# A decoder trunk with product-key experts on one core: stores of what ScalarE has written, issued by ScalarE instead of SyncE

## The chip, the cores and the metric

The kernel runs on one core of one Trainium2 chip. The metric is the time of one execution on the device in microseconds (us); less is better. PE is the matmul engine TensorE, DVE is VectorE, ACT is ScalarE, POOL is GpSimd and SP is SyncE, which has no arithmetic and here issues transfers only. Each of these engines works through a list of instructions of its own in the written order, and an instruction that waits holds everything behind it on that engine, the issue of transfers included.

## The reference

One layer of a decoder on 1024 tokens of width 1024, in float32. Two token mixers run beside each other (differential attention, and attention over 256 positions that an indexer selects), their outputs are gated and projected, an attention over 256 memory tokens is added, and then comes the channel mixer, in which most of the time goes:

```python
q = (hf @ w_q).reshape(n, PEER_HEADS, 2, PEER_HALF)              # 8 heads
sc = jnp.einsum('nhcd,hckd->nhck', q, sub_keys)                  # 2 x 128 keys a head
s_top, i_top = lax.top_k(sc, PEER_TOPK)                          # 16 + 16
...                                                              # best 16 of their sums
idx = best_i.reshape(n, PEER_HEADS * PEER_TOPK)                  # 128 of 16384 experts a token
g = jax.nn.softmax(best_s, axis=-1)
...
a = jnp.einsum('cd,ced->ce', hc, u[ic])
a = jax.nn.gelu(a, approximate=False) * gc
return jnp.einsum('ce,ced->cd', a, v[ic])
```

A residual sum and an rms norm end it.

## The kernel before

The tokens lie in eight blocks of 128, in two groups of four. Each group goes through the same phases: P (projections, from which some results are spilled to HBM), T (both attentions; a side lane "fill" computes the gates and, in the first group, the keys and values of the memory), G and O (gating and output product), M (memory attention) and R (the experts' scores, stored to HBM as pq). After phase R of the first group its blocks 0 to 3 are served by gathers: POOL fetches 128 rows of u and 128 rows of v per block by index, 512 each in all, and DVE multiplies them (L1031, L1050). These gathers are spread over the rest of the program as a lane of their own.

The blocks of the second group, 4 to 7, are not gathered. `dense` runs all 128 tiles of 128 experts over them. It has two stages.

The early stage makes the first 48 U products. For each, SP loads a tile uraw (512 KB, three buffers), ACT and DVE split it into a high and a low part uT (L106, L107, two buffers), PE does 24 matmuls into one accumulator (L129 to L131), ACT applies the gelu (two buffers) and the result is stored to ga (256 KB, L1219). Beside it runs the lane "weights", which finds for each of the four blocks the chosen experts ("route"), transposes them (L1124, L1125), makes bit codes of them (L1144, L1145) and then, four tokens at a time in 32 iterations a block, the table of all experts' weights: a product dot, oh by ACT (L1161), ah by DVE (L1163), a product out, and a copy by ACT into wbuf (L1169). A wbuf holds half a block (64 tokens), and there are two. Each half is stored to Wd by eight stores of 512 KB (L1177), put into a list when the half is done and taken from it one by one in the steps that follow, or all at once where the next half of a block needs it.

The main stage then goes through all 128 expert tiles in groups of four. `group` loads the weights wl from Wd (L1237), and c from ga (L1241) or makes it by a U product, and multiplies the two; `second` loads V (vraw, L1256), splits it and makes the second product (L129 to L131 again, into kept and out).

A scheduler sets the order of the instructions on each engine from the order of the code, the lanes' times and its own costs, and lays down which buffers wait for what. Before the change every transfer of `dense` and nearly all others are issued by SP. A Wd store is put behind the last u load that was issued when it was recorded (`issue_after`). Eight semaphores mark the end of transfers; SP's and ACT's transfers take them in turn, and an issue also waits for the transfer that had the same semaphore before.

Of the kernel before, what the change touches and what calls it, by code (L numbers as in the profile page):

```python
# [78 lines left out]
class K:  # L79
# [245 lines left out]
    def phase_P(self, g, st, hp, hT):  # L325
        nc, a = self.nc, self.a
        blks = self.blks
        w_in = a["w_in"][0]
        with ExitStack() as ctx:
# [5 lines left out]
            for i, b in enumerate(blks):  # L335
                x = pp.tile([P, D], F32, name="x", bufs=X_BUFS[g])
                nc.sync.dma_start(x, a["x"][0, b * P:(b + 1) * P])
                h = pp.tile([P, D], F32, name="h", bufs=X_BUFS[g])
# [121 lines left out]

            def use_dav(i, b, o):
                t = copy(o, 512)
                nc.sync.dma_start(self.dav[b], t)

            self.daq = self.scratch([4, 2, 2, 64, self.GT], f"daq{g}")
            self.dsq = self.scratch([self.GB, 64, 2, 2, 512], f"dsq{g}")
# [38 lines left out]
    def gates(self, g, hT):  # L505

        nc = self.nc
        for c in range(0, 16, 2):
            yield from self.fill(self.a["w_in"][0], KD, C_GATE + c * P, 256, 2, self.by_col(hT), self.GT, len(hT) == 1)
            for j in range(2):  # L510
                t = self.fp.tile([P, 512], F32, name="fout", bufs=2)[:, :self.GT]
                nc.scalar.activation(t, self.filled[j][:, :self.GT], AF.Tanh, bias=self.gb[:, c + j:c + j + 1], scale=0.5)
                self.gate[g, c + j] = self.scratch([P, self.GT], f"G{g}_{c + j}")
                nc.sync.dma_start(self.gate[g, c + j], t)

    def rope_view(self, d, s, b, groups):
        nc = self.nc
# [273 lines left out]
    def memory_kv(self):  # L791
        nc, w = self.nc, self.a["w_mem_kv"][0]
        self.mkd = self.scratch([P, 4, 256], "mkd")
        self.mvd = [self.scratch([P, 512], f"mvd{i}") for i in range(2)]
        for c in range(0, 4, 2):
            yield from self.fill(w, KD, c * P, 256, 2, self.by_col(self.memT), 256)
            for j in range(2):
                t = self.fp.tile([P, 512], F32, name="fout", bufs=2)
                nc.scalar.activation(t[:, :256], self.filled[j][:, :256], AF.Copy)
                nc.sync.dma_start(self.mkd[:, c + j], t[:, :256])  # L800
        yield from self.fill(w, KD, 512, 512, 2, lambda k, x, j: ([t[:, k, j * P:(j + 1) * P] for t in self.memT], x), 512)
        for i in range(2):
            t = self.fp.tile([P, 512], F32, name="fout", bufs=2)
            nc.scalar.activation(t, self.filled[i], AF.Copy)
            nc.sync.dma_start(self.mvd[i], t)

    def queries_M(self, g, x1, q, hp):
        nc, a = self.nc, self.a
# [54 lines left out]
    def phase_R(self, g, x1, rh, fp):  # L863
        nc, a = self.nc, self.a
        with ExitStack() as ctx:
# [17 lines left out]
            for half in range(2):  # L883
                po = self.product([(a["peer_w_q"][0], half * 512, 512)], KD, 512, self.by_column(T), self.GT, 4)
                for j in range(0, 4, 2):
# [6 lines left out]
                    for i in range(self.GB):  # L892
                        o = self.acc()
                        for hh in range(2):
                            nc.tensor.matmul(o[:, hh * 256:(hh + 1) * 256], qs[hh][:, i * P:(i + 1) * P],
                                             keysT[:, h + hh], start=True, stop=True)
                        so = rp.tile([P, 512], F32, name="so", bufs=3)
                        nc.scalar.activation(so, o, AF.Copy)
                        nc.sync.dma_start(self.pq[self.blks[i]][h // 2], so)
                    self.pace.tick(4 * 0.9)  # L900


# [206 lines left out]
    def weights(self, blks):  # L1109

        nc = self.nc
# [5 lines left out]
        for j, b in enumerate(blks):  # L1117
# [30 lines left out]
            for n0 in range(0, P, 4):  # L1148
# [24 lines left out]
                if m + 4 == H:  # L1173
                    for e0 in range(0, P, 16):
                        def store(e0=e0, at=2 * j + n0 // H, wbuf=wbuf):
                            with self.tc.issue_after(self.last_load):
                                nc.sync.dma_start(self.Wd[at, :, e0:e0 + 16], wbuf[:, e0:e0 + 16])  # L1177
                        stores.append(store)
        while stores:
            stores.pop(0)()  # L1180
# [2 lines left out]
    def dense(self, psum, early):  # L1183
# [5 lines left out]
        with ExitStack() as ctx:  # L1189
# [20 lines left out]
            with ExitStack() as c2:  # L1210
# [3 lines left out]
                for e in range(early):  # L1214
# [1 line left out]
                    t = self.wb.tile([P, 512], F32, name="gelu", bufs=2)  # L1216
                    nc.scalar.activation(t, o, AF.Gelu)
                    ga[e] = self.scratch([P, 512], f"ga{e}")
                    nc.sync.dma_start(ga[e], t)  # L1219
                self.pace.drain("weights")  # L1220
            self.route_ctx.close()
            psum = self.psum_phase(psum, "ps3", A_BUFS)
# [199 lines left out]
```

## Time and profile before

| | |
|---|---|
| Time, median of three runs | 3506.32 us (3500.16, 3506.32, 3507.83) |
| The profiled execution | 3504.34 us |
| Its span (first to last instruction) | 3502.6 us |
| Mean granted clock of PE | 0.932 of full speed |
| PE busy | 3011.4 us, 86% of the span |
| DVE busy | 2853.1 us, 81% |
| ACT busy | 1398.2 us, 40% |
| POOL busy | 1389.4 us, 40% |
| Transfers issued by SP (the hardware queue) | 401.94 MB, 33.7% of the span of the 16 transfer engines |
| Gathers by POOL | 560.01 MB, 45.3% |

The first 640 us are the first group, 640 to about 1640 us the second, 1640 to 2241 us the early stage of `dense`, and the rest is its main stage. The issuing of transfers does not count as an engine's busy time. Where a row tells of a wait, the time in brackets is the engine's idle time just before the instruction, and behind the arrow stands what ended it.

### The profile page before, as it was taken

How to read it: one execution, taken by the hardware profiler on the slowest of the kernel's cores; microseconds unless marked ns; L12 is line 12 of the kernel's file. 1: busy time of each engine (PE TensorE's matmuls, PEld its weight loads, DVE VectorE, ACT ScalarE, POOL GpSimd, SP SyncE). 2: the span in 40 equal slices, each digit the busy share in tenths (PEclk: the TensorE clock that was granted, in tenths of full speed). 3: DMA queues.
4: the chain of work that ended last, by engine and by line, in shares of the span. 5: the costliest groups of instructions: out<-in, count | busy, mean ns of one | idle time of the engine just before them, and what ended most of it. 6: DMA issues, size and time to landing. Idle time of an engine off the chain costs nothing. (4 is left out here: it accounts for less than half of the span.)

```text
span 3502.6 us, 42276 instructions
## 1 busy us (share of the span) xinstructions
PE 3011.4 (86%) x13234; PEld 2283.0 (65%) x13234; DVE 2853.1 (81%) x6623; ACT 1398.2 (40%) x2537; POOL 1389.4 (40%) x1122
## 2 busy tenths in 40 slices
PE   8999888798687698676899895588899999999997
PEld 7777766553355575455677674466677888787886
DVE  6656554598878979888999888677789999899998
ACT  5756344245666441322546465222222222222222
POOL 0010000011245246653122665424457665777665
PEclk9999989899899799788999998799999999999999
DMA  4575544335799579897486999999999999999997
GB/s 138 163 186 133 169 138 142 124 121 192 210 296 297 143 262 362 296 327 277 149 296 219 364 377 346 369 302 319 307 340 368 380 381 367 364 364 387 376 381 285
DMA packets 394210, 964.64 MB, mean 275 GB/s; under 512 B 36713, under 2 KB 146049, under 8 KB 392577
## 3 DMA queue, kind: packets, MB, share of 16 engines
q0 software_dynamic: 155264, 560.01, 45.3%
q1 hardware_dynamic: 238720, 401.94, 33.7%
q8 instruction: 104, 1.70, 0.2%
q14 instruction: 122, 0.99, 0.1%
HBM read 871.64 MB, written 90.18 MB: 275 GB/s over the span
## 5 line engine op out<-in xcount | busy, mean ns | idle before, releaser
L1028 POOL DMA_INDIRECT rows<-in_peer_u_dram,ii x512 | 673.8, 1316 | 920.8 <-DVE rows L1031 377.0
L1044 POOL DMA_INDIRECT rows<-in_peer_v_dram,ii x512 | 651.0, 1272 | 438.9 <-DVE h3s L1050 286.2
L1050 DVE SCALAR_TENSOR_TENSOR h3s<-rows,wexp,h3s 128x1024 f32<-128x1024 f32 x508 | 651.1, 1282 | 38.9 <-DMA rows<-in_peer_v_dram,ii 29.4
L1031 DVE SCALAR_TENSOR_TENSOR rows<-rows,h3s 128x1024 f32<-128x1024 f32 x512 | 611.9, 1220 | 81.5 <-DMA rows<-in_peer_u_dram,ii 80.0
L129 PE MATMUL acc<-fT,uT 128*128 128x512 f32 x1024 | 415.7, 406 | 46.3 <-ACT uT L106 26.0
L131 PE MATMUL acc<-fT,uT 128*128 128x512 f32 x1024 | 413.5, 404 | 11.8 <-DVE uT L107 11.5
L130 PE MATMUL acc<-fT,uT 128*128 128x512 f32 x1024 | 410.2, 401 | 0.0
L106 ACT ACTIVATE c<-wl 128x512 fp32r<-128x512 f32 x128 | 80.2, 631 | 817.1 <-PE out L130 407.8
L143 POOL TENSOR_TENSOR rstd<-msq,mhalf 128x1 f32<-128x1 f32 (+1 forms) x42 | 35.6, 847 | 597.4 <-DVE msq L141 578.6
L129 PEld LDWEIGHTS acc<-fT,uT 128*128 128x128 f32 x1024 | 197.0, 192 | 92.2 <-ACT uT L106 26.8
L131 PEld LDWEIGHTS acc<-fT,uT 128*128 128x128 f32 x1024 | 197.0, 192 | 66.7 <-DVE uT L107 21.0
L130 PE MATMUL kept<-v,c 128*128 128x512 f32 x512 | 206.2, 405 | 38.8 <-DVE v L107 38.8
L129 PE MATMUL kept<-v,c 128*128 128x512 f32 x512 | 202.6, 402 | 37.6 <-ACT v L106 36.2
L106 ACT ACTIVATE uT<-uraw 128x1024 fp32r<-128x1024 f32 x128 | 135.5, 1059 | 245.4 <-PE acc L130 135.0
L130 PEld LDWEIGHTS acc<-fT,uT 128*128 128x128 f32 x1024 | 197.2, 193 | 39.2
L107 DVE TENSOR_TENSOR w<-wraw,w 128x512 fp32r<-128x512 f32 (+1 forms) x176 | 116.7, 680 | 117.9 <-ACT w L106 111.2
L129 PE MATMUL out<-v,c 128*128 128x512 f32 x512 | 203.9, 398 | 9.7 <-DVE accu L1274 9.7
L131 PE MATMUL kept<-v,c 128*128 128x512 f32 x512 | 203.4, 397 | 0.0
L130 PE MATMUL out<-v,c 128*128 128x512 f32 x512 | 203.0, 396 | 0.0
L131 PE MATMUL out<-v,c 128*128 128x512 f32 x512 | 202.8, 396 | 0.0
L562 ACT ACTIVATE junk<-W,xb 128x384 bf16<-128x384 f32 (+5 forms) x186 | 163.8, 881 | 77.3 <-DVE xb L560 67.8
L127 PE MATMUL acc<-wraw,hT 128*128 128x512 f32 (+1 forms) x384 | 168.4, 592 | 14.1 <-ACT tok L349 10.9
(361 smaller groups left out, 6691.5 us busy)
## 6 DMA issues: line engine op xcount, KB each, us to landing
uraw<-in_peer_ut_dram SPq DMA_DIRECT2D x128, 512.0 KB
vraw<-in_peer_v_dram SPq DMA_DIRECT2D x128, 512.0 KB
Wd<-wbuf SPq DMA_DIRECT2D x64, 512.0 KB
wl<-Wd SPq DMA_DIRECT2D x64, 512.0 KB
wraw<-in_w_in_dram SPq DMA_DIRECT2D x40, 512.0 KB
fraw<-in_w_in_dram SPq DMA_DIRECT2D x32, 512.0 KB
wraw<-in_w_out_dram SPq DMA_DIRECT2D x24, 512.0 KB
ga<-gelu SPq DMA_DIRECT2D x48, 256.0 KB
```

The lines of the kernel that those rows point to most:

```text
L106: self.nc.scalar.activation(hi, src, AF.Copy)
L107: self.last_dve = self.nc.vector.tensor_tensor(lo, src, hi.bitcast(F32), op=OP.subtract).ins
L127: self.last_pe = nc.tensor.matmul(out, l[0], r[0], start=start, stop=stop).ins
L129: nc.tensor.matmul(out, l[0], r[0], start=start, stop=False)
L130: nc.tensor.matmul(out, l[0], r[1], start=False, stop=False)
L131: self.last_pe = nc.tensor.matmul(out, l[1], r[0], start=False, stop=stop).ins
L143: nc.gpsimd.tensor_tensor(r, v, self.mhalf[:, :n], op=OP.pow)
L562: nc.scalar.activation(junk[:, :(b + 1) * P], self.W[b], AF.Sign, bias=xb[:, j:j + 1].bitcast(F32), accum_out=s[:, j:j + 1])
L1028: nc.gpsimd.indirect_dma_start(out=u, out_offset=None, in_=a["peer_u"][0], in_offset=bass.IndirectOffsetOnAxis(ap=ii[:, j:j + 1], axis=0))
L1031: nc.vector.scalar_tensor_tensor(u, u, 1.0, h3, op0=OP.mult, op1=OP.mult, accum_out=aa[:, j:j + 1])
L1044: nc.gpsimd.indirect_dma_start(out=v, out_offset=None, in_=a["peer_v"][0], in_offset=bass.IndirectOffsetOnAxis(ap=r["ii"][:, j:j + 1], axi ...
L1050: nc.vector.scalar_tensor_tensor(o, v, w[:, j:j + 1], o, op0=OP.mult, op1=OP.add)
```

## The change

190 stores whose data ACT has written are issued by ACT (`nc.scalar`) instead of SP (`nc.sync`): 8 of dav, 32 of the gates, 4 and 2 of the memory's keys and values, 32 of pq, 64 of Wd and 48 of ga. The Wd stores lose their place behind the last u load. The spilled queries and keys, x2, h3 and the output stay with SP, and so do all loads. Nothing that is computed changes.

```diff
             def use_dav(i, b, o):
                 t = copy(o, 512)
-                nc.sync.dma_start(self.dav[b], t)
+                nc.scalar.dma_start(self.dav[b], t)
...
                 self.gate[g, c + j] = self.scratch([P, self.GT], f"G{g}_{c + j}")
-                nc.sync.dma_start(self.gate[g, c + j], t)
+                nc.scalar.dma_start(self.gate[g, c + j], t)
...
                 nc.scalar.activation(t[:, :256], self.filled[j][:, :256], AF.Copy)
-                nc.sync.dma_start(self.mkd[:, c + j], t[:, :256])
+                nc.scalar.dma_start(self.mkd[:, c + j], t[:, :256])
...
             nc.scalar.activation(t, self.filled[i], AF.Copy)
-            nc.sync.dma_start(self.mvd[i], t)
+            nc.scalar.dma_start(self.mvd[i], t)
...
                         nc.scalar.activation(so, o, AF.Copy)
-                        nc.sync.dma_start(self.pq[self.blks[i]][h // 2], so)
+                        nc.scalar.dma_start(self.pq[self.blks[i]][h // 2], so)
...
                         def store(e0=e0, at=2 * j + n0 // H, wbuf=wbuf):
-                            with self.tc.issue_after(self.last_load):
-                                nc.sync.dma_start(self.Wd[at, :, e0:e0 + 16], wbuf[:, e0:e0 + 16])
+                            nc.scalar.dma_start(self.Wd[at, :, e0:e0 + 16], wbuf[:, e0:e0 + 16])
                         stores.append(store)
...
                     ga[e] = self.scratch([P, 512], f"ga{e}")
-                    nc.sync.dma_start(ga[e], t)
+                    nc.scalar.dma_start(ga[e], t)
```

The scheduler writes the order anew, so the change shows in three places of the early stage. In the listings a number behind a name tells apart the tiles of one name, x2 or x8 stands for so many rows alike, and after the change the lines from L1177 on have numbers one lower.

First listing, before: SP's queue at the second half of the third block (wbuf_17520), up to the last of five u loads.

```order
L1196 DMA uraw_18246<-in_peer_ut_dram 128x1024
L1177 DMA Wd_13635<-wbuf_17520 128x1024 x2
L1219 DMA ga43_17980<-gelu_17978 128x512
L1177 DMA Wd_13635<-wbuf_17520 128x1024 x3
L1219 DMA ga44_18068<-gelu_18066 128x512
L1177 DMA Wd_13635<-wbuf_17520 128x1024 x3
L1219 DMA ga45_18143<-gelu_18141 128x512
L1196 DMA uraw_21052<-in_peer_ut_dram 128x1024
L1196 DMA uraw_21098<-in_peer_ut_dram 128x1024
L1196 DMA uraw_21146<-in_peer_ut_dram 128x1024
```

The same place of SP's queue after the change, and on to the first loads of the main stage.

```order
L1195 DMA uraw_18246<-in_peer_ut_dram 128x1024
L1195 DMA uraw_21052<-in_peer_ut_dram 128x1024
L1195 DMA uraw_21098<-in_peer_ut_dram 128x1024
L1195 DMA uraw_21146<-in_peer_ut_dram 128x1024
L1195 DMA uraw_21189<-in_peer_ut_dram 128x1024
L1195 DMA uraw_21395<-in_peer_ut_dram 128x1024
L1236 DMA wl_18902<-Wd_13635 128x8x128
L1240 DMA c_18904<-ga0_13695 128x512
```

The stores have left the queue: the u loads follow each other, and the two u loads of the main stage that stood between the last Wd stores and wl before (uraw_21441, uraw_21486) now come behind the first loads of V.

Second listing, before: ACT in the last block, where its first half (wbuf_18422) is done and the second (wbuf_18655) begins.

```order
L1169 ACTIVATE wbuf_18422<-out_18641 128x4x128
L1161 ACTIVATE oh_18674<-dot_18670,m6_13636 128x512
L1161 ACTIVATE oh_18688<-dot_18684,m6_13636 128x512
L1169 ACTIVATE wbuf_18655<-out_18678 128x4x128
L1161 ACTIVATE oh_18702<-dot_18698,m6_13636 128x512
L1169 ACTIVATE wbuf_18655<-out_18664 128x4x128
```

The same place after the change.

```order
L1169 ACTIVATE wbuf_18422<-out_18641 128x4x128
L1161 ACTIVATE oh_18674<-dot_18670,m6_13636 128x512
L1176 DMA Wd_13635<-wbuf_18422 128x1024 x3
L1161 ACTIVATE oh_18688<-dot_18684,m6_13636 128x512
L1161 ACTIVATE oh_18702<-dot_18698,m6_13636 128x512
L1176 DMA Wd_13635<-wbuf_18422 128x1024 x5
L1169 ACTIVATE wbuf_18655<-out_18678 128x4x128
L1169 ACTIVATE wbuf_18655<-out_18664 128x4x128
```

The eight stores of the first half have moved in among the steps of the second half's first iterations, in pieces of 3 and 5.

Third listing, before: PE at the transposes of the last block's experts (L1124, L1125). acc_18252 is the last of the 48 U products, acc_17988 the third before it.

```order
L129 MATMUL acc_18252<-fT0_12993,uT0_18248 128x512
L130 MATMUL acc_18252<-fT1_12994,uT0_18248 128x512
L131 MATMUL acc_18252<-fT0_12993,uT1_18249 128x512
L1124 MATMUL out_18371<-ident_66,ids_18351 128x128
L1125 MATMUL out_18371<-ident_66,gw_18364 128x128
L1144 MATMUL out_18388<-ident_66,bi_18378 112x128 x4
```

The same transposes on PE after the change.

```order
L129 MATMUL acc_17988<-fT0_12993,uT0_17984 128x512
L130 MATMUL acc_17988<-fT1_12994,uT0_17984 128x512
L131 MATMUL acc_17988<-fT0_12993,uT1_17985 128x512
L1124 MATMUL out_18371<-ident_66,ids_18351 128x128
L1125 MATMUL out_18371<-ident_66,gw_18364 128x128
L129 MATMUL acc_18076<-fT0_12993,uT0_18072 128x512
```

The transposes have moved ahead of the last three U products; the codes' first transposes (L1144) now stand ahead of the last two.

## Rows read from the trace of the kernel before

**Rows 1.** Page: the span, and busy us (share) and instructions by engine

```profile
span 3502.6 us, 42276 instructions
PE 3011.4 (86%) x13234; PEld 2283.0 (65%) x13234; DVE 2853.1 (81%) x6623; ACT 1398.2 (40%) x2537; POOL 1389.4 (40%) x1122
```

**Rows 2.** Stretches: length, PE, PEld, DVE, ACT, POOL busy, PE clock, DMA share, GB/s

```profile
2241.00:3502.00 1261.00, 1167.16 (x4944) 946.39 (x4944) 1134.32 (x1406) 330.11 (x433) 734.15 (x545) 0.96 0.97 351
1640.00:2241.00 601.00, 489.76 (x2547) 382.09 (x2546) 518.87 (x1526) 309.22 (x393) 234.99 (x187) 0.93 0.80 295
1820.00:1840.00 20.00, 15.80 (x73) 12.27 (x72) 20.00 (x93) 5.55 (x10) 2.84 (x2) 0.99 0.71 245
1940.00:2000.00 60.00, 47.37 (x194) 36.62 (x193) 44.36 (x82) 16.91 (x22) 35.86 (x25) 0.91 1.02 407
2100.00:2140.00 40.00, 16.48 (x72) 12.55 (x71) 26.54 (x38) 10.19 (x15) 18.93 (x15) 0.66 0.95 361
1900.00:2241.00 341.00, 251.23 (x1338) 197.49 (x1336) 272.27 (x358) 168.93 (x214) 192.75 (x154) 0.89 0.97 367
```

**Rows 3.** Waits of SP's queue, 1640 to 2215: us in total, times, longest

```profile
SPq L1219 <- ACT gelu L1217: 154.9, 32, 15.0
SPq L1177 <- ACT wbuf L1169: 100.0, 8, 43.9
```

**Rows 4.** Timelines of ACT, PE, DVE: start, us, instruction, idle time before and its end

```profile
1814.22 1.06 ACT L106 ACTIVATE uT<-uraw 128x1024 fp32r<-128x1024 f32 x1 [5.57 <-DMA uraw<-in_peer_ut_dram]
1968.01 1.06 ACT L106 ACTIVATE uT<-uraw 128x1024 fp32r<-128x1024 f32 x1 [11.31 <-DMA uraw<-in_peer_ut_dram]
2114.30 1.06 ACT L106 ACTIVATE uT<-uraw 128x1024 fp32r<-128x1024 f32 x1 [11.29 <-DMA uraw<-in_peer_ut_dram]
2123.30 1.93 PE L1144 MATMUL out<-ident,bi 128*112 128x128 f32 x8 [18.68 <-DVE bi L1139]
2237.51 0.69 DVE L1245 TENSOR_TENSOR wl<-c,wl 128x512 f32<-128x512 f32 x1 [10.02 <-DMA c<-ga]
2241.77 0.79 PE L129 MATMUL kept<-v,c 128*128 128x512 f32 x1 [33.91 <-ACT v L106]
```

**Rows 5.** Timeline of SP's queue in the early stage: start, us, issues

```profile
1750.09 7.96 SPq L1177 DMA_DIRECT2D Wd<-wbuf  x8
2041.67 9.18 SPq L1177 DMA_DIRECT2D Wd<-wbuf  x8
2095.51 5.29 SPq L1196 DMA_DIRECT2D uraw<-in_peer_ut_dram  x3
2164.78 43.63 SPq L1177 DMA_DIRECT2D Wd<-wbuf  x16
2203.05 3.91 SPq L1177 DMA_DIRECT2D Wd<-wbuf  x2
2208.51 6.34 SPq L1196 DMA_DIRECT2D uraw<-in_peer_ut_dram  x2
```

**Rows 6.** Timeline of PE: two matmuls of a U product that follow each other

```profile
2103.78 0.39 PE L130 MATMUL acc<-fT,uT 128*128 128x512 f32 x1
2104.01 0.40 PE L131 MATMUL acc<-fT,uT 128*128 128x512 f32 x1
```

**Rows 7.** Timelines of SP's queue and PE at the turn to the second group

```profile
648.17 0.42 SPq L337 DMA_DIRECT2D x<-in_x_dram  x1
658.09 1.94 PE L156 MATMUL tps<-ident,h 128*128 128x128 f32 x8 [13.84 <-DVE h L148]
```

**Rows 8.** Stores by line: ns of an issue (least/median/most), first and last start

```profile
L1177 SPq DMA_DIRECT2D Wd<-wbuf x64: 319/894/2377, 1750.1 to 2207.0; - x64
L1219 SPq DMA_DIRECT2D ga<-gelu x48: 319/320/1498, 1650.6 to 2118.5; - x48
```

**Rows 9.** Timeline of ACT in the last block, behind its first half

```profile
2167.78 0.69 ACT L1161 ACTIVATE oh<-dot,m 128x512 f32<-128x512 f32 x1 [2.57 <-PE out L1167]
```

**Rows 10.** Page: DVE's products of gathered rows of u, busy us and mean ns

```profile
L1031 DVE SCALAR_TENSOR_TENSOR rows<-rows,h3s 128x1024 f32<-128x1024 f32 x512 | 611.9, 1220 | 81.5 <-DMA rows<-in_peer_u_dram,ii 80.0
```

## The prediction

> **What bounds the kernel now.** I read the page first: PE is busy for 86% of the span and every other engine for less [rows 1], so a queue's time counts only where PE stands still because of it. The table of stretches says where that is. From 2241 us to the end PE is busy 1167 of 1261 us [rows 2]: PE sets the pace, and the change touches nothing there, because every moved store lies earlier. In the early expert stage (1640 to 2241 us) PE is busy 490 of 601 us [rows 2]: 111 us are open. ACT, which gets the stores, is busy 309 of these 601 us, so there is room on the average, and the question is what stands in line behind a store.
>
> Then the waits of SP's queue in that stage. SP stood 154.9 us at the gelu stores until ACT had written the data, and 100.0 us at the Wd stores until wbuf was written [rows 3]. Loads stand behind these. What that costs is seen where ACT, the first user of a u tile, waits for the tile: 5.57, 11.31 and 11.29 us [rows 4], each time just after the second half of a block has been stored. DVE and PE stand behind ACT there: PE is idle for 4.2 us of the stretch 1820 to 1840, for 12.6 us of 1940 to 2000 and for 23.5 us of 2100 to 2140 (20 − 15.80, 60 − 47.37, 40 − 16.48 [rows 2]), 40.3 us in three places.
>
> **The sum, part by part.** It is made against the profiled execution, 3504.3 us, of which 3502.6 are span [rows 1]; the median of the runs is 3506.3, that is 2.0 us more.
>
> (a) *Loads of u that no longer stand behind Wd and ga stores.* The third place, around 2100, is the clearest. SP issues eight Wd stores of a second half in pieces of 2, 3 and 3 between gelu stores, and three u loads come behind them at 2095.51 [rows 5]. In the changed order these three stand directly behind other u loads (first listing), so only a free buffer holds them. Not all of the 23.5 us comes back: PE's wait at 2123.30 was for DVE's codes of the next block (18.68 us [rows 4]), and DVE came to them late partly for its own reasons. The changed order puts that block's transposes three U products ahead and its first codes two (third listing), so that two U products remain to fill the gap: one of their matmuls starts every 0.23 us [rows 6], and 2 × 24 × 0.23 is 11.0 us. I take 12, one of it for the load. In the first two places the DMA engines were busy for 0.71 and 1.02 of the stretch [rows 2], so that a load issued earlier takes its share of the same engines from stores and gathers. I take half of 4.2 + 12.6, that is 8.4. Together 20; bounds 0 (the transfers bound) and 40.3.
>
> (b) *Turn into the main expert loop.* Ahead of the first loads of Wd and of the stored gelus, SP issues two u loads that take 6.34 us [rows 5]. DVE then waits 10.02 us for c, and PE stands 33.91 us before its first product with V [rows 4]. In the changed order those two loads come behind the first loads of v, so c comes some 6 us sooner. Gain 6; bounds 0 (wl waits for the last Wd store instead) and 10.02.
>
> (c) *The other stores, off SP.* At the turn to the second group x is loaded at 648.17, behind scores that are stored, and PE stands 13.84 us [rows 7]. A load that is one or two issues earlier is worth some 2 us; bounds 0 and 5. The other gaps of the first 1640 us that I followed end at stores which stay on SP, so nothing is credited there.
>
> (d) *64 Wd stores on ACT.* Each held SP's queue for 0.319 to 2.377 us, median 0.894 [rows 8]: 57 us in all, and that is ACT's time now. Each waits for ACT's own last write to wbuf, which is just done, and, as on SP, for the earlier transfer that used the same of eight completion semaphores. Queued behind it are the oh and wbuf of the next iterations, the gelus, and the hi parts of u; DVE waits for the last, PE for all of them. There are four kinds of place.
> - Last block, between its halves: eight stores in two pieces, 3 and 5, stand among the steps that make oh and wbuf (second listing). PE has no U products left to cover them, only the small products that wait for just these steps. A burst of eight took 7.96 us on SP at 1750 and 9.18 at 2041 [rows 5]; I take 8.6. ACT stood 2.57 us at that point anyhow [rows 9]: 6 us lost.
> - First halves of the other three blocks: a burst of eight each (first and last of the three in [rows 5]), while PE has two U products in hand, 11.0 us. Covered when both tiles are ready; 2 us each for where they aren't: 6. Without the cover it is 8.6 each, 26 in all.
> - Second halves of those blocks: 24 stores, about one behind every ACT step, where ACT is half idle: 3 us; 21 (24 × 0.894) if none of it is covered.
> - Last eight: PE has only the gap of 33.91 us ahead of it, in which ACT waits too. 0; if wl came later by a whole burst it would be 8.6.
> Sum 15; bounds 5 and 62 (6 + 26 + 21 + 9).
>
> (e) *48 ga stores on ACT*, 0.320 us at the median [rows 8], 15.4 us in a stage where ACT has 292 us free: 1 us, bounds 0 and 5 (a third of it on the path).
>
> (f) *78 stores of dav, gates, memory and scores on ACT*, at the same 0.320 us 25 us over the first 1640, in which PE waits for other things most of the time: 2 us, bounds 0 and 8.
>
> No row shows a store that ACT issues, so the prices are SP's. Below nothing they cannot go, since ACT does each as an added instruction. Gained 20 + 6 + 2 = 28, lost 15 + 1 + 2 = 18: **10 us less, 3494 by the profiled run, 3496 by the median.**
>
> **Rivals.** *R1, slower: ACT is held by its own bursts.* Two stores at 2203.05 took 3.91 us on SP, 1.95 each [rows 5]. At that price a burst of eight is 15.6 us. It decides from the point where a burst outlasts the two U products that PE has in hand: 11.0 us, or 1.38 us a store. Beyond it each of three first halves costs 15.6 − 11.0 and the 2 of misfit, 20 for three; the tail 15.6 − 2.6 = 13; the second halves' 3 become 7 (1.95/0.894); (e) and (f) 3: 43 lost. Of the gains the loads' 8.4 is gone, because the same full engines hold them, so 20 is left: 23 us more, 3529. For it: transfers were busy 0.97 of 1900 to 2241 [rows 2]. Against it: the bursts of eight on SP stayed at 9.18 us and under. In "Perfetto Trace Analysis", section "DMA Instruction — HWDGE (DVE, Sync)", the Trainium skill says that one sequencer at a time has the descriptor generator to itself. By it a load on SP and a burst on ACT would hold each other up, which would raise the price towards R1; no row here shows two queues at it together.
>
> *R2, no change: the loads are late anyway.* With 1.02 in 1940 to 2000 and 0.95 in 2100 to 2140 [rows 2] the u loads share the engines with POOL's gathers, so an earlier issue brings no earlier tile. Left are the order's 11.0, and (b) and (c) at half, 4: 15 gained, 18 lost, 3509. Against it: in 1820 to 1840 there was room (0.71), and SP's issue was shut for 43.63 us in one row [rows 5], which is time for a producer and not for transfers. The Trainium skill's "DMA: Bandwidth & Descriptors", section "Issuing engines are not separate DMA queues", speaks for this rival: starting transfers from several engines saves only the sequencer's time, usually small beside the transfer. The row of 43.63 us does not agree with "small" for this queue; no run here has shown yet whether the transfers then come sooner.
>
> *R3, the order decides.* The scheduler has written PE and DVE anew from the first group on. Counted there, DVE does 12 more of its gather products ahead of phase O of the second group, 1220 ns each [rows 10]: 15 us brought forward, with 1024 in all as before. If it lands on the path and is not given back later, the forecast rises by 7 to 15, to 3503 or 3511. The other way, all of (a) to (c) comes free, 40.3 + 10 + 2 = 52, less 18: 3472, or 3464 with bursts that cost 10 in all.
>
> **How the numbers follow.** The forecast of 3496, with gains of 20 to 40 against losses of 10 to 25, gets 0.42; no change, by R2 or R3's dear form, 0.26; slower by R1, 0.28; much faster by R3's other way, 0.04. A measurement of this kernel can tell about 0.2%, 7.0 us, from no change: faster is below 3499.3, slower above 3513.3. So faster 0.46, same 0.26, slower 0.28. The range runs from 3464 to 3530: it takes in R2, R3 and R1 up to its price, and leaves out a dearer R1 (uncovered second halves too), 0.12, and still more gain, 0.05. The forecast's own range is 3480 to 3505.
>
> **What would show it.** (a): ACT's waits of 11 us for uraw behind second halves are gone, and PE's idle time in the early expert stage falls from 111 us to about 95. (b): the gap of 33.91 becomes about 28, with c issued ahead of the last two u loads. (d): bursts of eight on ACT take 8 to 9 us while U products go on; in the middle of the tail ACT shows one pause of about 6. If bursts are 15 us, or gaps of PE stand right behind them, it is R1; if u loads are issued early and land as late as before, R2. If the first 1640 us change by more than 5 us either way, the order decided, which no term prices. I would be wrong above all if a store on ACT waits for earlier transfers to be through, or if DVE and not the load held the places behind second halves.

## The result, and the profile after

The changed kernel takes 3546.02 us (median of four runs, 3539.12 to 3551.57), the kernel before 3504.7 us beside it. The ratio is 1.0107, with a 95% interval from 1.0085 to 1.0128: slower by some 37 to 41 us, where 10 us faster were forecast. The profiled execution took 3547.01 us. These lines of its page answer to [rows 1].

```profile
span 3545.2 us, 42120 instructions
PE 3032.0 (86%) x13234; PEld 2300.4 (65%) x13234; DVE 2854.6 (81%) x6623; ACT 1394.8 (39%) x2537; POOL 1378.5 (39%) x1122
```

The same work, and PE stands still for longer. To see where, I cut both traces at the same piece of work, not at the same time: where the second group's attention ends (its last product with the values, L720), where its scores end (last L895), where the table of weights ends (last L1167), and where the first product with V starts. All numbers in this table are starts of those matmuls, in us.

| | before | after |
|---|---|---|
| first attention score of the second group | 965.8 | 976.9 |
| end of its attention | 1284.7 | 1303.7 |
| end of its scores | 1614.4 | 1634.3 |
| end of the table of weights | 2196.7 | 2258.7 |
| first product with V | 2241.8 | 2280.1 |
| span | 3502.6 | 3545.2 |

So 19 to 20 us are lost by the end of the second group's attention, 42 more in the early expert stage, 24 come back at the turn into the main stage, and the main stage adds 4. The stretches between those marks show it too; columns as in [rows 2], the stage from the scores' end to the weights' end and the turn, first of after:

```profile
1634.30:2258.70 624.40, 489.79 (x2507) 382.52 (x2505) 533.06 (x1580) 304.10 (x392) 238.67 (x199) 0.90 0.78 287
2258.70:2280.10 21.40, 11.16 (x52) 8.90 (x50) 4.21 (x5) 5.83 (x7) 0.00 (x0) 0.83 0.93 333
```

and of the kernel before:

```profile
1614.40:2196.70 582.30, 481.88 (x2507) 375.10 (x2505) 512.44 (x1571) 307.55 (x392) 228.88 (x183) 0.94 0.80 292
2196.70:2241.80 45.10, 11.19 (x52) 8.93 (x50) 25.34 (x23) 5.91 (x7) 19.76 (x18) 0.67 1.02 388
```

In the stage PE's idle time went up from 100 to 135 us, and its granted clock went from 0.94 to 0.90 with it. The turn is shorter by 23.7 us. There POOL is busy for 0.00 us instead of 19.76, and the transfer engines moved 333 GB/s instead of 388.

The first thing that the prediction asked for did happen. ACT's waits for u tiles, from 1640 us to the first product with V, were (us in total, times, longest) before and after:

```profile
ACT uT L106 <- DMA uraw<-in_peer_ut_dram: 34.8, 6, 11.3
```

```profile
ACT uT L106 <- DMA uraw<-in_peer_ut_dram: 6.7, 3, 5.7
```

Counted from the scores' end, 1614 us, the first row would be 46.7 us. PE's wait for the codes of the next block (bi) shrank as well. Before (from 1640 us) and after (from 1660), in the same form, with PE's wait for ah below each:

```profile
PE out L1144 <- DVE bi L1139: 33.2, 6, 18.7
PE dot L1157 <- DVE ah L1163: 8.2, 7, 3.2
```

```profile
PE out L1144 <- DVE bi L1139: 19.5, 3, 9.8
PE dot L1157 <- DVE ah L1163: 46.5, 9, 13.0
```

So PE got back 13.7 us at the codes and lost 38.3 at ah.

Nor did ACT's issues turn out dearer than SP's. By line (ns of an issue, least/median/most) the median of a Wd store is below that of [rows 8]:

```profile
L1176 ACTq DMA_DIRECT2D Wd<-wbuf x64: 326/528/1927, 1760.8 to 2267.6; - x64
```

The lower median comes from stores that stand alone: the three bursts of eight that ACT issues in one piece take 8.74, 9.05 and 8.90 us, as on SP in [rows 5].

What stands instead is in PE's timeline: four new gaps, one in the middle of each block's table, and all wait for ah, which is DVE's. The fifth row is the turn, which was 33.91 us in [rows 4].

```profile
1784.06 1.01 PE L1157 MATMUL dot<-codes,code 112*128 112x512 bf16 x2 [9.02 <-DVE ah L1163]
1938.02 0.59 PE L1157 MATMUL dot<-codes,code 112*128 112x512 bf16 x1 [12.95 <-DVE ah L1163]
2097.52 0.58 PE L1157 MATMUL dot<-codes,code 112*128 112x512 bf16 x1 [10.02 <-DVE ah L1163]
2233.38 0.58 PE L1157 MATMUL dot<-codes,code 112*128 112x512 bf16 x1 [8.87 <-DVE ah L1163]
2280.10 0.80 PE L129 MATMUL kept<-v,c 128*128 128x512 f32 x1 [10.24 <-ACT v L106]
```

DVE's timeline ahead of the fourth gap shows why ah is late: nine gather products in a row stand between two ah.

```profile
2215.12 0.69 DVE L1163 SCALAR_TENSOR_TENSOR ah<-dot,gT 128x512 f32<-128x512 f32 x1
2215.72 5.24 DVE L1050 SCALAR_TENSOR_TENSOR h3s<-rows,wexp,h3s 128x1024 f32<-128x1024 f32 x4
2221.50 1.28 DVE L1050 SCALAR_TENSOR_TENSOR h3s<-rows,wexp,h3s 128x1024 f32<-128x1024 f32 x1 [0.54 <-DVE h3s L1050]
2223.98 1.28 DVE L1050 SCALAR_TENSOR_TENSOR h3s<-rows,wexp,h3s 128x1024 f32<-128x1024 f32 x1 [1.19 <-DMA rows<-in_peer_v_dram,ii]
...
2231.44 1.28 DVE L1050 SCALAR_TENSOR_TENSOR h3s<-rows,wexp,h3s 128x1024 f32<-128x1024 f32 x1 [1.21 <-DMA rows<-in_peer_v_dram,ii]
2232.64 0.68 DVE L1163 SCALAR_TENSOR_TENSOR ah<-dot,gT 128x512 f32<-128x512 f32 x1
```

The first four find their rows gathered and take 1.3 us each; the last four each wait for the next gather, and they come 2.48 us apart. From one ah to the next it is 17.5 us. In the order of the program there are runs of 10, 9 and 9 such products in the middle of the last three blocks, where the kernel before has at most 4; in the first of the four blocks it is four of them and 27 steps of the routing. These are the places where ACT's list now holds the eight stores of a first half. ACT's own rows there:

```profile
2209.31 1.36 ACTq L1176 DMA_DIRECT2D Wd<-wbuf  x3
2214.49 3.62 ACTq L1176 DMA_DIRECT2D Wd<-wbuf  x5
```

Eight stores in 5.0 us of issuing, all of it over by 2218.11, where the wait for ah goes on to 2233: ACT was not what PE waited for.

### The profile page after: what moved, and what is told of

The parts are those of the page before. It is cut to its first block, busy times and chain, and to the rows that moved or that the text cites. A ratio compares the mean times of both kernels' runs of the same rounds, so it can differ in the third digit from the quotient of the medians.

```text
span 3545.2 us, 42120 instructions
## 1 busy us (share of the span) xinstructions
PE 3032.0 (86%) x13234; PEld 2300.4 (65%) x13234; DVE 2854.6 (81%) x6623; ACT 1394.8 (39%) x2537; POOL 1378.5 (39%) x1122
## 4 chain that ended last, share of the span: by engine, by line
PE 32%; DVE 21%; issue 18%; DMA 16%; POOL 9%; ACT 4%; SPq 1%; ACTq 0%; POOLq 0%; DVEq 0%
POOL rows L1028 5%; PE acc L129 4%; PE acc L131 4%; PE acc L130 4%; DMA c<-ga 3%; DMA rows<-in_peer_v_dram,ii 3%; POOL rows L1044 3%; DMA rows<-in_peer_u_dram,ii 3%; DVE rows L1031 2%; DVE h3s L1050 2%; DMA so<-pq 2%; PE po L720 2%; DMA fraw<-in_w_in_dram 2%; PE fill L127 1%; PE kept L130 1%
## 5 line engine op out<-in xcount | busy, mean ns | idle before, releaser
L1044 POOL DMA_INDIRECT rows<-in_peer_v_dram,ii x512 | 640.6, 1251 | 502.8 <-DVE h3s L1050 338.8
L129 PE MATMUL out<-v,c 128*128 128x512 f32 x512 | 203.8, 398 | 11.1 <-DVE accu L1273 7.3
L1167 PEld LDWEIGHTS out<-ah,oh 128*128 128x128 f32 x1024 | 147.2, 202 | 83.7 <-issue 59.4
```

What stands on the lines that cost most here:

```text
L129: nc.tensor.matmul(out, l[0], r[0], start=start, stop=False)
L1044: nc.gpsimd.indirect_dma_start(out=v, out_offset=None, in_=a["peer_v"][0], in_offset=bass.IndirectOffsetOnAxis(ap=r["ii"][:, j:j + 1], axi ...
L1167: nc.tensor.matmul(o[:, i], oh[:, i], ah[:, i], start=True, stop=True)
```

## Experiments: queue or order

**Theory O**: the scheduler's new order costs the time. **Theory I**, the prediction's R1: issuing on ACT holds ACT up. Both orders can be had with both queues, since every instruction has the same name in both programs. The names of one program's instructions, engine by engine, are laid down in the other as edges of issue order (no wait for an end), and only the stores that change queues are left to the scheduler. Each ratio below is taken against runs of the kernel before made beside it, whose median lay between 3499 and 3504 us; so two experiments are best compared by their ratios.

```diff
+def pin(tc):      # ORDERS: one list of names per engine
+    for names in ORDERS:
+        for last, name in zip(names, names[1:]):
+            tc.add_manual_dep(ins[name], last, NoSync, reason="pin")
...
         trunk(tc, a, out)
+        pin(tc)
```

The change's stores in the order of before (`act_order_before`), and once more for its trace (`act_order_before_2`):

> The stores are issued by ACT as in the change, but PE, DVE, POOL, ACT's arithmetic and all loads keep, word for word, the order that they have in the kernel before; only the place of the stores in ACT's list is the scheduler's. Theory O (the new order costs the time, above all the runs of nine and ten gather products that DVE's list now holds between two ah at the half blocks): nothing of the 41 us is left, 3490 to 3512 us, and the PE gaps of 9 to 13 us behind ah are gone. Theory I (issuing on ACT holds ACT up, the prediction's R1): the loss stays, 3535 to 3555 us, with gaps of PE behind the bursts of eight stores.

> The same program as the run with the order of before and the stores on ACT, for a trace at the higher clock. Expected again 3510 to 3520 us, that is 10 to 19 above the kernel before. Theory: with this order the cost is ACT's own time in the bursts of eight stores, seen as gaps of PE of 3 to 7 us right behind each of the four first halves (some 20 us), less what the u loads gain. If the cost lies ahead of 1640 us, it is the 78 other stores instead.

3515.49 us, ratio 1.0042 (1.0024 to 1.0059), and the second time 3510.13 us, 1.0031 (1.0018 to 1.0045).

The stores on SP in the order of after (`sp_order_after`):

> The reverse: the stores stay with SP as before, but PE, DVE, POOL, ACT's arithmetic and all loads have the order of the changed kernel; only the place of the stores in SP's list is the scheduler's. Theory O: the loss comes with the order alone, 3530 to 3560 us, with the PE gaps behind ah at the half blocks. Theory I: near the kernel before, 3495 to 3515 us.

3548.03 us, ratio 1.0139 (1.0116 to 1.0162). The new order with the old queue has all of the loss; whether it has a little more is not settled, since the interval overlaps that of the change. Its PE gaps are the same ones, behind the same ah; the last three of four:

```profile
1948.74 2.08 PE L1167 MATMUL out<-ah,oh 128*128 128x128 f32 x8 [12.82 <-DVE ah L1163]
2106.11 0.58 PE L1157 MATMUL dot<-codes,code 112*128 112x512 bf16 x1 [13.75 <-DVE ah L1163]
2240.93 1.22 PE L1167 MATMUL out<-ah,oh 128*128 128x128 f32 x4 [12.99 <-DVE ah L1163]
```

So theory O holds for the most part. Theory I has a remainder of 11 to 15 us in the order of before, and the second trace shows it where the prediction had put it: right behind ACT's bursts of eight PE stands still, in each of the four blocks.

```profile
1753.21 1.01 PE L1167 MATMUL out<-ah,oh 128*128 128x128 f32 x3 [5.77 <-ACT wbuf L1169]
1900.61 0.58 PE L1157 MATMUL dot<-codes,code 112*128 112x512 bf16 x1 [4.08 <-ACT oh L1161]
2054.82 0.59 PE L1157 MATMUL dot<-codes,code 112*128 112x512 bf16 x1 [8.19 <-ACT oh L1161]
2183.92 1.01 PE L1167 MATMUL out<-ah,oh 128*128 128x128 f32 x3 [3.86 <-ACT wbuf L1169]
```

The first two bursts on ACT in that trace:

```profile
1744.12 1.65 ACTq L1176 DMA_DIRECT2D Wd<-wbuf  x3
1745.89 6.19 ACTq L1176 DMA_DIRECT2D Wd<-wbuf  x5
...
1888.87 7.85 ACTq L1176 DMA_DIRECT2D Wd<-wbuf  x8
```

They take 7.84 and 7.85 us, and the four gaps are 21.9 us together. From the scores' end to the weights' end that trace has 604.0 us, 21.7 more than before. The whole is only 11 to 15 us longer: in this one trace the scores end 7.8 us earlier than before (1606.6). That these stores and no others make up the remainder was the question of the next run: ga and the 78 others on ACT, Wd on SP, order of before (`pin_ga78`).

> ga and the 78 other stores on ACT (126), Wd on SP, every engine's order as in the kernel before. Theory: without bursts a store on ACT costs next to nothing, and the second group gains some us from loads that no longer stand behind stores; 3490 to 3500 us. With Wd on ACT as well in the same order it was 3510 to 3515 us, so the 64 Wd stores would account for all of that. If single stores on ACT cost 0.33 us each on the path: 3510 us or more.

3497.95 us, ratio 0.9990 (0.9977 to 1.0002), not to be told from no change. 126 stores on ACT cost nothing and gain nothing that can be measured; the 64 Wd stores account for the rest. The run does not try what earlier u loads are worth: with Wd on SP, ACT still waits 33.2 us for u tiles in its trace.

## Experiments: the runs of gather products

`after_spread` keeps the change's order and moves the products alone.

```diff
 # DVE's list, in the middle of each of the last three blocks (g: a gather product)
-ah g g g g g g g g g ah g ah g ah ...
+ah g ah g g ah g g ah g g ...
```

> The changed kernel with its own order on all queues, but for one thing: of the three runs of 10, 9 and 9 gather products that DVE's list has between two ah in the middle of the last three blocks, one product stays and the others follow one by one behind the next ah's. Theory O: the three PE gaps of 13, 10 and 9 us (32 together) shrink to under 3 us each; since the products still have to be done beside the same iterations, some 15 to 30 us come back: 3515 to 3530 us. Theory I: no change against the changed kernel, 3540 to 3552 us.

3526.27 us, ratio 1.0066 (1.0046 to 1.0086): 14 us back by the ratios and 20 by the medians, and the gaps at 1938, 2097 and 2233 are gone. But of these gaps' 31.8 us the stage got back only 8.6 (615.8 us instead of 624.4): PE's wait for ah fell from 46.5 to 18.2 us, that for oh rose from 20.5 to 29.0. The runs as such are thus the smaller part of the stage's loss. The rest of this gain lies in the main stage, whose length differs by some 14 us from trace to trace (1251 to 1265 us). `after_no_flush` takes away what calls for the runs, the burst itself:

```diff
                 if n0 % H == 0:
-                    while stores:
+                    while n0 == 0 and stores:
                         stores.pop(0)()
```

> The changed kernel, but the eight stores of a first half are no longer issued all at once where the second half begins; one goes out behind each of the iterations that follow, as those of the second half do. The scheduler is free, and its DVE list then holds no run of more than five gather products between two ah. Theory O: the stores come in a burst, the scheduler takes ACT for blocked in it and fills DVE with gather products; without the burst the gaps at the half blocks go, 20 to 30 us back: 3512 to 3525 us (the second group's 20 us stay). If the number of stores on ACT and not the burst costs the time: 3535 to 3550 us.

3510.97 us, ratio 1.0037 (1.0025 to 1.0050): 25 us back by the ratios and 35 by the medians, with all 190 stores still on ACT. In its trace, which is of its fastest run, the stage takes 583.7 us, about as long as before the change (582.3), and the turn 38.3. So the stage's loss goes with the burst: where the order is kept, by ACT's own time in it (the four gaps above); where the scheduler is free, by the order that it writes around the burst. How much of the latter is the filling of DVE, beyond what the run above gave back, is not shown. That the scheduler takes ACT for blocked longer than it is, 9 or 10 products of 1.28 us being some 12 us against bursts of 5.0 to 9.05 measured, is argued from the order and not shown either.

`dense_no_flush` moves only Wd and ga, without the burst:

```diff
-                nc.sync.dma_start(ga[e], t)
+                nc.scalar.dma_start(ga[e], t)
 # Wd as in the change, the burst as above; the 78 others stay with SP
```

> Only the stores of the early expert stage (Wd and ga) are issued by ACT, without the burst; the 78 others stay with SP. The second group keeps the order of the kernel before, so its 20 us should not appear. Theory O: what is left is the change's gain, 3485 to 3500 us, faster than the kernel before, with the wait of 33.9 us ahead of the main stage near 10. If stores on ACT cost more than loads on SP gain: 3505 to 3520 us.

3506.58 us, ratio 1.0011 (0.9994 to 1.0029): the loss is gone, but the gain that I expected isn't there. Its trace, of a run of 3512.74 us, has 599.2 us in the stage and 37.4 in the turn.

The turn: `u_behind_v` is the kernel before with two loads moved in SP's list, and all else pinned.

```diff
 # SP's list
 Wd<-wbuf x8
-uraw_21441, uraw_21486
 wl_18902, c_18904, wl_18918, vraw x2, c, vraw x2, c
+uraw_21441, uraw_21486
```

> The kernel before in its own order on every engine, with stores on SP; only the two u loads that stand between the last Wd stores and the first loads of the main stage are moved behind the first loads of V. This is the prediction's term (b) alone: the wait for c of 10.0 us gone and the gap of 33.9 us 6 us shorter, 3492 to 3498 us. If wl or V end the gap in any case: no change, 3498 to 3503 us.

3502.33 us, ratio 1.0014 (1.0001 to 1.0027). The gap is still 31.83 us. Without those loads SP's next issues took longer: the first c 8.80 us instead of 5.05, the first two loads of V 12.02 instead of 11.24:

```profile
2228.49 12.02 SPq L1256 DMA_DIRECT2D vraw<-in_peer_v_dram  x2
...
2243.30 0.69 DVE L1245 TENSOR_TENSOR wl<-c,wl 128x512 f32<-128x512 f32 x1 [9.18 <-DMA c<-ga]
```

(the first row is SP's, the second DVE's timeline). What went with the shorter turn in the changed kernel is seen in its stretch above: no gathers at all in it, since their products had been done ahead of it. With the stores on SP and the same order the turn is as short:

```profile
2265.95:2287.30 21.35, 11.18 (x51) 8.94 (x50) 4.41 (x6) 5.84 (x7) 0.00 (x0) 0.84 0.93 321
```

With the runs spread it is 21.5 us and has no gathers either; without the bursts it is 38.3, with 12 of POOL's instructions in it, where the kernel before has 18 in 45.1. Part of what the products cost in the stage was thus given back there.

## Experiments: the second group

`only_78` moves only the stores ahead of the early stage.

```diff
 # dav, gates, mkd, mvd, pq as in the change
 # Wd and ga stay with nc.sync
```

> Only the 78 stores ahead of the early expert stage (dav, gates, memory keys and values, scores) are issued by ACT; Wd and ga stay with SP as before; the scheduler is free. Of the 41 us that the change costs, about 20 were there by 1600 us, ahead of the early stage. If they come from these stores and what the scheduler makes of them: 3515 to 3530 us, with the delay at the end of the second group near 20. If the order of the second group is changed by the dense stores as well, or by chance: anything from 3495 to 3530, the delay at 1600 us not 20.

3512.98 us, ratio 1.0027 (1.0013 to 1.0041); in its trace the attention ends at 1301.8, 17 us late; in the changed kernel it is 19. In the order of before the same stores on ACT cost nothing (above), so this half is the order as well. My first idea was R3's: the twelve gather products that DVE does more ahead of phase O. It was tried twice. `gathers_both` put the products of the second group where the kernel before has them, in a list that is otherwise the change's:

```diff
 # DVE's list: as in the run with the runs spread, and in the second group
 # each product behind as many other instructions as in the kernel before
```

> The changed kernel with its own order on PE, ACT and SP and its stores on ACT; two things are moved in DVE's list alone: the three runs of 9 and 10 gather products are spread as in the run before, and in the second group the gather products stand where the kernel before has them (182 instead of 194 ahead of phase O). POOL's order is left to the scheduler. Theory O, both halves of the loss come from where gather products stand: the 20 us that the spreading gave back and another 12 to 18 us for the second group, 3502 to 3514 us. If the second group is slower for another reason than those 12 products: 3520 to 3530 us.

3566.85 us, ratio 1.0191 (1.0178 to 1.0204), slower than the change itself. A placement that is foreign to the rest of the order made new waits (the attention ends at 1330.0), so this run settles nothing. `only_78_held` is gentler: the scheduler stays free, but the products may not come sooner.

```diff
+def hold(tc):     # HELD: an instruction, and the products that may not be issued ahead of it
+    for anchor, products in HELD:
+        for n in products:
+            tc.add_manual_dep(ins[n], anchor, NoSync, reason="hold")
```

> As the run with only the 78 stores on ACT (3513 us, 18 us late by 1600 us), the scheduler free, with one thing added: at each sum of phase T and at the first sum of phase O of the second group, no more gather products may stand ahead in DVE's list than in the kernel before (102 instead of 114 at the end of the differential attention, 182 instead of 194 at phase O). Theory O, the twelve products brought forward, 1.28 us each, are the second group's loss: 3495 to 3503 us, no delay at 1600 us. If the second group is slower for another reason in the order or by ACT's issues: 3509 to 3517 us as before.

3519.49 us, ratio 1.0055 (1.0038 to 1.0072). With the whole change and no bursts (`no_flush_held`, the same lines in it):

> All 190 stores on ACT as in the change, without the bursts, and with the gather products of the second group held as in the run above. This joins the two remedies. Theory O: 3511 us less the second group's 11 to 18, 3493 to 3502 us, as fast as the kernel before or a little faster. If the second group's loss is not those products: 3508 to 3515 us.

3513.83 us, ratio 1.0039 (1.0023 to 1.0055). No gain in either: the twelve products are not it. That theory fell.

What else is new in that order shows in the stretches up to the first attention score, for the gates' tile alone (columns as in [rows 2], without DVE and POOL); before and after:

```profile
640.00:965.77 325.77, 50.48 (x94) 18.91 (x94) 2.75 (x4) 0.90 0.55 169
```

```profile
640.00:976.92 336.92, 61.34 (x120) 23.47 (x120) 3.99 (x6) 0.91 0.57 184
```

26 more matmul records of the gates (13 products), 10.9 us of PE, stand ahead of the score; the score is 11.1 us late. Inside the attention more gates stand ahead as well, so that they run out sooner: their last matmul starts at 1089.6 and the attention's last score at 1159.6, 70 us with nothing of the gates beside the attention. Before, these were 1099.6 and 1140.6, 41 us. **Theory G**: the gates came forward, and the attention's chain waits behind them on PE. `only_78_fills` holds them, and nothing else, in the form shown above:

```diff
+# HELD: a product of the second group's attention, and the gates' products that the kernel before has behind it
```

> Only the 78 stores on ACT, as before (3513 us), the scheduler free; added: at the products of the second group's attention no more products of the gates may stand ahead on PE than in the kernel before (47 instead of 60 ahead of the first score, 26 matmul records fewer). Gather products are not held (194 ahead of phase O). Theory G, gates brought forward keep the attention's chain waiting: 3495 to 3503 us, no delay left at 1300 us. If it is something else in that order: 3509 to 3517 us.

3483.07 us, ratio 0.9954 (0.9937 to 0.9971): 26 to 30 us less than without the hold (by the ratios and by the medians), and 16 less than the kernel before. Its stretch:

```profile
640.00:962.87 322.87, 49.54 (x94) 18.34 (x94) 3.40 (x5) 0.91 0.54 178
```

The attention ends at 1275.0. The same hold in the whole change (`after_fills`) and in the change without bursts (`no_flush_fills`):

> The whole change (3541 to 3546 us) with the same hold of the gates' products in the second group. Theory G: the second group's 18 to 20 us go and the early stage's loss stays, 3518 to 3528 us. Otherwise: 3538 to 3548 us.

> The whole change without the bursts of Wd stores (3511 us) and with the gates' products held. Theory G and theory O together: 3490 to 3500 us, all of the loss gone, perhaps a little faster than the kernel before. Otherwise 3508 to 3515 us.

3508.33 us, ratio 1.0021 (1.0006 to 1.0036), and 3483.71 us, ratio 0.9956 (0.9940 to 0.9971). All three are faster than expected. The stage of the first is 624.1 us, as in the change without the hold, so the two losses are separate. Theory G is shown by three kernels, each of which gains some 26 to 38 us by adding these edges alone; the scheduler orders the rest anew around them. Why they gain more than the loss is not tried apart. Two things go with it: the scheduler puts even fewer gates ahead than the kernel before has, 95 against 100 products at the middle of the scores; and PE stands less at the gates' products for their own weights (fraw). In the kernel before, with only the 78, and with these and the hold, from 640 to 1310 us:

```profile
PE fill L127 <- DMA fraw<-in_w_in_dram: 27.1, 3, 14.5
PE fill L127 <- DMA fraw<-in_w_in_dram: 24.9, 4, 10.2
PE fill L127 <- DMA fraw<-in_w_in_dram: 6.5, 3, 4.7
```

What waits behind such a product waits with it, the attention's products too.

Is the 16 us gain the queue's after all? `sp_order_fills` keeps that order and gives the 78 stores back to SP:

```diff
 # kernel before, pinned to the order of the run with the gates held
```

> All stores on SP as in the kernel before, but PE, DVE, POOL, ACT's arithmetic, the loads and the other stores in the order of the run with 78 stores on ACT and the gates' products held (3483 us). If that order alone is the gain: 3480 to 3490 us. If the queue of the 78 stores is (loads on SP that no longer stand behind stores): 3496 to 3506 us. In between, both.

3487.88 us, ratio 0.9963 (0.9945 to 0.9982): nearly all of it is the order's. The last run moves ga too (`ga78_fills`), as the version that the others point to:

```diff
 # as the run with the gates held, and
-                    nc.sync.dma_start(ga[e], t)
+                    nc.scalar.dma_start(ga[e], t)
```

> 126 stores on ACT (ga and the 78), Wd on SP, the gates' products held, the scheduler free: the version that the runs so far point to, since the Wd bursts were the only stores on ACT that cost. Theory: ga costs nothing on ACT and its u loads gain little, 3478 to 3488 us. If the gelu stores on SP were what kept the u loads late: below 3478 us.

3479.73 us, ratio 0.9939 (0.9917 to 0.9961): the lowest median of all, 21 us below the kernel before. Its interval overlaps that of the run without ga, so what ga adds is not settled. Its early stage is little changed against the kernel before, 573 us instead of 582, with the turn as long as ever:

```profile
1602.30:2175.40 573.10, 479.22 (x2505) 373.63 (x2504) 506.73 (x1560) 307.17 (x392) 215.13 (x178) 0.93 0.79 292
2175.40:2221.00 45.60, 11.22 (x51) 8.97 (x49) 25.41 (x23) 5.95 (x8) 19.46 (x18) 0.65 1.03 388
```

## Why the prediction was wrong, point by point

- **The step that failed** is the sum itself: it was made as if the order stayed, with one piece of the new order added as a gain. What it had no term for are DVE's gather products between two ah, which PE waited for (46.5 us instead of 8.2), and the gate products ahead of the attention, by which the second group ended 19 to 20 us late. The order of before under the new queue costs 0.3 to 0.4%, the new order under the old queue 1.4%.
- **What bounds the kernel** was read rightly as far as the rows went: PE, with SP's queue shut in the early stage. The step from there, that PE's idle time behind ACT's load waits comes back when the waits go, failed. ACT's waits fell from 34.8 to 6.7 us and PE's idle time in the stage rose from 100 to 135.
- **(a)**, 20 us, came true in its larger part and was outweighed. The transposes did move, and PE's wait for the codes, 18.68 us in its longest, fell to 9.80, in all from 33.2 to 19.5. But the same order had put runs of nine and ten gather products into DVE's list, and I priced only the piece of it that I showed. The smaller part, for earlier loads, is not seen apart: in the order of before ACT's waits for u tiles fell to 16.6 us, and PE waited 26.0 us for ACT's part of u in all, as in the kernel before.
- **(b)**, 6 us, failed as a mechanism: moving those two loads alone gave nothing. The turn did become shorter, by 23.7 us, with gathers done sooner, which no term had.
- **(c)** cannot be told from zero.
- **(d)**, 15 us, was right in place for an order that stays, and too small in size: the four gaps are 21.9 us where first halves and the tail were priced at 12. That the kernel as a whole came to 11 to 15 us is luck, since its trace is ahead of the kernel before when the stage begins. In the order that was really run, the eight stores in the tail took 5.0 us and not 8.6, and the gap there was DVE's. **(e)** and **(f)** were right: nothing to be seen.
- **R1** named the sign and, for the changed kernel, the wrong cause: bursts stayed at 9.05 us and under, where it needed more than 11.0. **R2** said 3509, and moving all stores in the old order comes to 3510 to 3515; but its sum holds 11.0 us for a new order that these runs do not have, so the agreement is luck. The Trainium skill's "DMA: Bandwidth & Descriptors", section "Issuing engines are not separate DMA queues", says that starting transfers from several engines saves only the sequencer's time. The 126 stores agree: moved to another engine, they changed the time by 0.1% (interval 0.23% less to 0.02% more).
- **R3** said that the order decides, and it did. I gave its dear form 7 to 15 us and let it end at no change, since I had counted one thing in it, gather products ahead of phase O. Holding those back gained nothing. The two that cost, 13 gate products ahead of the attention and the order around the bursts with its three runs of gather products, could be read in the order beforehand.

## What to carry to other kernels

Where a scheduler writes the order, a change of queue is a change of order. Before summing durations, read the new order at every chain that bounds a stage, for work of low priority that has moved ahead of it, on each engine and not on one. To tell the two apart, pin the old order under the new queue and the new order under the old queue. A burst of issues on an engine that also computes is best dealt out one by one between its steps; here that gave 25 to 35 us back, 190 stores still on ACT.

## What was not expected

- A gather product costs DVE 1.28 us while rows are in store and 2.48 us when it has to wait for each gather (rows above), so that a run of nine is 17.5 us from ah to ah and not the 12 that its instructions add up to.
- The median issue of a Wd store was 528 ns on ACT in the changed kernel, 894 on SP before ([rows 8]) and 982 on ACT in the order of before; a burst of eight in one piece took 7.85 to 9.05 us on ACT in these two traces, and 7.96 and 9.18 on SP ([rows 5]). With the bursts dealt out (`after_no_flush`) the median is 327 ns, so a store that stands alone costs a third of one in a burst. Why a burst is dear was not tried.
- With gathers in it the turn took 45.1 us, at 388 GB/s and a transfer share of 1.02; without them 21.4. With the two u loads moved behind them, the loads that stood first in SP's queue were nearly as late (9.18 us of waiting for c instead of 10.02). That full transfer engines and not the queue held them is the likeliest reading; no run changed the gathers of the turn alone.
- Why the scheduler brings the gates forward when their stores leave SP, and whether a hold on the gates with a still smaller number gains more, is open.
